# RWKV-7 time mixing: weight halves and modulation tiles issued in fixed slots behind each engine's last short operation

## The chip, the cores and the metric

The kernel runs on one NeuronCore of a Trainium2 chip. The metric is the device time of one execution in microseconds (us); the median of three runs before the change is 2659.18 us.

Engines as the profile names them: PE is the matrix engine (PEld its weight loads), DVE the vector engine, ACT the scalar engine, POOL is GpSimd, SP the queue that issues nearly all DMAs. PSUM is the memory PE writes to, SBUF the on-chip memory for everything else.

## The reference, cut to what matters

A trunk of two layers over 256 tokens of width 2048, all in float32. Layer 0 is RWKV-7 time mixing and a squared-ReLU MLP; layer 1 is attention and an MLP. Each sub-layer has a norm, a shift and scale from the conditioning vector `c`, and a gate. The change lies in layer 0's time mixing:

```python
mod = c @ w_ada[layer] + b_ada[layer]            # 12288 modulation values a layer, from a 2048 x 12288 matrix
sh1, sc1, gt1, sh2, sc2, gt2 = jnp.split(mod, 6, axis=-1)
...
xr, xw, xk, xv, xa, xg = [h + xx * mu[j] for j in range(6)]
r = xr @ w_r;  k = xk @ w_k;  v = xv @ w_v       # three 2048 x 2048 projections
...
def step(S, inp):                                # the recurrence of each of 32 heads, one token at a time
    r_t, w_t, k_t, v_t, kk_t, a_t = inp
    sa = jnp.einsum('bhvk,bhk->bhv', S, -kk_t)
    S = (S * w_t[:, :, None, :] + sa[..., None] * (kk_t * a_t)[:, :, None, :]
         + v_t[..., None] * k_t[:, :, None, :])
    return S, jnp.einsum('bhvk,bhk->bhv', S, r_t)
...
y = group_norm(y) + sum(r_h * k_h * r_k) * v_h
return (y * g) @ w_o
```

## The kernel before, in words

**Pairs and slots.** The 32 heads are worked as 16 pairs of two heads (128 channels). The recurrence is done in chunks of 64 tokens, so each pair needs a chain of small matrix products. Its work is a generator of 36 steps: `early` (8 steps: decay, key norm, scaled keys), `invert` (12 steps: the inverse of a triangular matrix, in levels l = 1 to 5, two steps a level) and `late` (16 steps: four chunks of three steps, then the group norm and gate). The loop at the end of `layer_a` runs over 164 slots, 8 a pair: in a slot each live pair takes one step, then PE gets a piece of dense work, two steps of the k and r projections of the next pair (12 matmuls of 128x256). In steady state four or five pairs are live, each at another place of its 36 steps. In this text phase 0 to 7 means the slot's number modulo 8, and a pair period is eight slots, from phase 0 to phase 0. One slot's results on ACT, DVE and POOL feed the next slot's matmuls.

**The short chains.** A step of `invert` transposes `u` on DVE (`tt`, line 243), PE multiplies it with a level mask of `als` (tile `al`), ACT copies the product (`xs`, line 247), PE multiplies that with `u`, and DVE adds the result to `u` (line 258). A chunk in `late` goes through PE, ACT (`g`, line 288; `sa`, line 292) and DVE (`zs`, lines 309 and 311).

**The long operations.** A float32 weight comes in halves of 512 KB (tile `raw`, a ring of 6 buffers), and is split in two parts: ACT casts it to `wH` (line 382), DVE subtracts for `wL` (line 385); `wH` and `wL` have 3 buffers each. The projections need four halves a pair (two of `w_k`, two of `w_r`); `self.weight` asks for both halves of a matrix at once, one matrix ahead. In the same slots the modulation vectors of later stages are computed: `self.ada()` takes one 512 KB tile of `w_ada` from the same ring of 6 and adds it, times a value of `c`, to an accumulator on DVE (`acc`, line 460; 458 for the first tile of 16), in phases 0, 1, 2, 4, 5, 6, from slot 16 on.

**What sets the order.** Each engine's instructions are ordered by a scheduler at build time, with priority for what was written first. `tc.issue_after(ins)` forces instructions of the same engine behind `ins`; before the change it is used for PE alone. Each engine works its own queue off in order. On PSUM the tile `ms` (two buffers) is shared by many short products: `z` (phase 0), the turned keys (1), the variance sums (1), the last inversion level (2 and 3), the key sums (2) and the gate (3).

Of the kernel before, what the change touches and what calls it, by code (L numbers as in the profile page):

```python
# [15 lines left out]
ALU = mybir.AluOpType  # L16
AX = mybir.AxisListType

P = 128
D = 2048  # L20
T = 256
KT = D // P
DFF = 8192
NQ = DFF // D
NPAIR = D // P
C = 64
H = C // 2
# [3 lines left out]
HK = 8  # L31
# [46 lines left out]
class Pair:  # L78
# [118 lines left out]
    def invert(self):  # L197
        b, nc, s, ch, kr, bh, kh = self.b, self.b.nc, self.s, self.ch, self.kr, self.bh, self.kh
        cst, pp = b.cst, b.pp

        def every(name):
            return cst(name).unsqueeze(1).to_broadcast([P, 4, H])

        def half(name, bufs):
            return b.pw.tile([P, 4, H], F32, tag=name, bufs=bufs, name=name)


        ui = cst("ui").unsqueeze(1).to_broadcast([P, 4, P])
        ts = []
        for src in (bh, kh):  # L210
            t = s()
            nc.gpsimd.tensor_tensor(out=ch(t), in0=ch(src), in1=self.pc.to_broadcast([P, 4, C]), op=ALU.mult)
            ts.append(t)
        pg = pp.tile([P, 4, P], F32, tag="gr", bufs=1, name="gr")
        self.each(lambda c: pg[:, c, :], lambda c: ch(bh)[:, c, :], lambda c: kr[:, c, :])
        ar = self.ar = s("ar", 3)
        nc.vector.tensor_tensor(out=ch(ar), in0=pg[:, :, C:P], in1=ui[:, :, C:P], op=ALU.mult)


        da, co, u = half("da", 1), half("co", 2), half("u", 2)  # L220
        for i, K in enumerate(QS):
            n = H * (i % 2)
            nc.scalar.copy(da[K], pg[K, :, n:n + H])
            if i % 2 == 0:
                nc.scalar.mul(co[K], pg[K, :, H:C], -1.0)
        nc.gpsimd.tensor_tensor(out=u, in0=da, in1=every("lev0"), op=ALU.mult)
        nc.gpsimd.tensor_tensor(out=u, in0=u, in1=every("eye_h"), op=ALU.add)
        als = b.pw.tile([P, 4, 4, H], F32, tag="al", bufs=2, name="al")
        nc.gpsimd.tensor_tensor(out=als, in0=da.unsqueeze(1).to_broadcast([P, 4, 4, H]),
                                in1=cst("levs").rearrange("p (l k) -> p l k", l=4).unsqueeze(2).to_broadcast([P, 4, 4, H]),  # L230
                                op=ALU.mult)
        yield
        pt = b.psm().rearrange("p (a c k) -> p a c k", a=2, c=4)
        for i, t in enumerate(ts):
            self.each(lambda c: pt[:, i, c, :], lambda c: ch(t)[:, c, :], lambda c: cst("eye"))
        bk = self.bk = b.pw.tile([P, 2, 4, C], F32, tag="bk", bufs=3, name="bk")
        nc.scalar.copy(bk, pt)
        yield
        uf = self.u = b.uf[self.j % 2]
        down, up = ((0, 1), (2, 3)), ((1, 0), (3, 2))  # L240
        for l in range(1, 6):
            tt_, xs = half("tt", 2), half("xs", 2)
            nc.vector.transpose(out=tt_.rearrange("p c t -> p (c t)"), in_=u.rearrange("p c t -> p (c t)"))
            pi = self.corner(l)
            if l < 5:
                self.tiles(pi, als[:, l - 1], tt_, [(i, i) for i in range(4)])
                nc.scalar.copy(xs, pi)
            else:
                self.tiles(pi, co, tt_, down)
                for i, K in enumerate(QS):  # L250
                    if i % 2:
                        nc.scalar.copy(xs[K], pi[K])
                    nc.gpsimd.tensor_copy(uf[K, :, H * (i % 2):H * (i % 2) + H], u[K])
            yield
            pi = self.corner(l)
            if l < 5:
                self.tiles(pi, xs, u, [(i, i) for i in range(4)])
                nc.vector.tensor_tensor(out=u, in0=u, in1=pi, op=ALU.add)
            else:
                self.tiles(pi, xs, u, up)  # L260
                for K in QS[::2]:
                    nc.scalar.copy(uf[K, :, H:C], pi[K])
            if l == 2:
                pg = pp.tile([P, 4, P], F32, tag="gr", bufs=1, name="gr")
                self.each(lambda c: pg[:, c, :], lambda c: ch(kh)[:, c, :], lambda c: kr[:, c, :])
                mk = self.mk = self.big("mk", 3)
                nc.vector.tensor_tensor(out=mk, in0=pg, in1=ui, op=ALU.mult)
            yield

    def late(self):  # L270
# [6 lines left out]
        zs = None  # L277
        for c in range(4):
            if c == 3:
                lg = pw.tile([P, 2, P], F32, tag="lg", bufs=1, name="lg")  # L280
                nc.sync.dma_start(out=lg, in_=b.d["lora2"][j, :, 2:4])
            g, sa = (pw.tile([P, C], F32, tag=n_, bufs=3, name=n_) for n_ in ("g", "sa"))
            for K in heads:
                mm(pch[K, 0, :], mk[K, c, 0:C], vp[K, c, :], start=True, stop=(c == 0))
            if c:
                for K in heads:
                    mm(pch[K, 0, :], kr[K, c, 0:C], zs[K, :], start=False, stop=True)
            nc.scalar.copy(g, pch[:, 0, :])
            yield
            for K in heads:  # L290
                mm(pch[K, 1, :], u[K, c, :], g[K, :], start=True, stop=True)
            nc.scalar.mul(sa, pch[:, 1, :], -1.0)
            yield
            for K in heads:
                mm(ch(py)[K, c, :], vp[K, c, :], mk[K, c, C:P], start=True, stop=False)
            if c:
                for K in heads:
                    mm(ch(py)[K, c, :], zs[K, :], kr[K, c, C:P], start=False, stop=False)
            for K in heads:
                ins = mm(ch(py)[K, c, :], sa[K, :], ch(ar)[K, c, :], start=False, stop=True)  # L300
            if c < 3:
                with b.tc.issue_after(ins.ins):
                    for K in heads:
                        mm(pch[K, 2, :], bk[K, 0, c, :], sa[K, :], start=True, stop=False)
                    for K in heads:
                        mm(pch[K, 2, :], bk[K, 1, c, :], vp[K, c, :], start=False, stop=True)
                zn = pw.tile([P, C], F32, tag="zs", bufs=4, name="zs")
                if c == 0:
                    nc.vector.tensor_copy(zn, pch[:, 2, :])
                else:  # L310
                    nc.vector.scalar_tensor_tensor(out=zn, in0=zs, scalar=pc[:, c, :], in1=pch[:, 2, :],
                                                   op0=ALU.mult, op1=ALU.add)
                zs = zn
            yield

# [18 lines left out]
class Body:  # L334
# [7 lines left out]
    def cst(self, name, rows=slice(None)):  # L342
        o, n = CST_AT[name]
        return self.csts[rows, o:o + n]
# [148 lines left out]
    def ada(self, n=1):  # L493
        for _ in range(n):
            self.ada_step()
        self.ada_fill()

    def last_pe(self):
        pe = self.nc.tensor.engine
# [140 lines left out]
    def layer_a(self, st, sp):  # L640
# [8 lines left out]
        with ExitStack() as s1:  # L649
# [137 lines left out]
            for n in range(KT):  # L787
# [19 lines left out]
                t = mixed(5, n, xx)  # L807
# [17 lines left out]
            for _ in range(2):  # L825
                v_part()
            s3.close()
            weights = iter([d[n][j] for j in range(NPAIR) for n in ("w_k", "w_r")])
            self.wnext = self.weight(next(weights))
            for i in range(4):  # L830
                nc.scalar.copy(v[:, 2 * i:2 * i + 2, :], pv[i])
            nc.scalar.activation(tw[:96, :], pl[0][:96, 0, :], AF.Tanh)
# [8 lines left out]
        with ExitStack() as s1:  # L841
# [13 lines left out]

            def proj_steps(pr):
                for dst, hl in (("k", xk), ("r", xr)):
                    w = self.wnext
                    src = next(weights, None)
                    self.wnext = None if src is None else self.weight(src)  # L860
                    ps = pp.tile([P, 2 * T], F32, tag="pj", bufs=2, name="pj")[:, :T]
                    for kt in range(KT):
                        self.proj(ps, w, lambda kt: hl[:, kt, :, 0:T], (kt, kt + 1))
                        if dst == "r" and kt == 1:
                            pr.lw = pw.tile([P, 2, P], F32, tag="lw", bufs=1, name="lw")
                            nc.sync.dma_start(out=pr.lw, in_=d["lora2"][pr.j, :, 0:2])
                        if kt % 2 == 1:
                            if kt == KT - 1:
                                t = pw.tile([P, T], F32, tag=dst, bufs=2, name=dst)
                                nc.scalar.copy(t, ps)  # L870
                                setattr(pr, dst, t)
                            yield
# [25 lines left out]
            for slot in range(S * NPAIR + Pair.STEPS):  # L898
# [24 lines left out]
                with tc.issue_after(last):  # L923
                    for _ in range(todo):
                        next(dense, None)
                if slot >= 2 * S and slot % 4 < 3:
                    self.ada()
            self.fin(HK)
        return v

# [311 lines left out]
```

## Time and profile before

| what | value |
|---|---|
| runs before | 2659.18, 2659.95, 2654.15 us (median 2659.18) |
| profiled execution | a span of 2653.8 us; no time of its own is given beside it |
| PE, DVE, ACT, POOL busy over the span | 97%, 79%, 52%, 8% |
| the loop over slots | from about 202 us to 733 us of the span; steady from 304 to 622 us |
| in the steady part (317.29 us) | PE busy 301.32, DVE 261.74, ACT 186.41, POOL 88.98 us |

How to read it: a row of the timeline has start, duration, engine, line, operation, output<-input, shape and count, and in brackets how long the engine sat idle before it and what ended that. A row of waits has who waited for whom, and then the us in total, how many times and the longest. A row of windows has the stretch, its length and each engine's busy time in it.

### The profile page before, as it was taken

The numbers are of one execution on the slowest core, as the hardware profiler recorded it, in microseconds if no ns is written. First come the engines' busy times: TensorE is split into PE (matmuls) and PEld (weight loads), VectorE is DVE, ScalarE is ACT, GpSimd is POOL, SyncE is SP. The second block draws the span as 40 slices with busy tenths as digits, with TensorE's granted clock in tenths as the row PEclk, the third lists the DMA queues.
The fourth block names the chain that finished last, engine by engine and source line by source line (L and its number), as shares of the span: only waits on it lengthen the run. The fifth ranks groups of instructions, "written<-read, shape, count | busy, mean of one in ns | idle before, by whom it ended". The sixth has DMA issues, their size and how long they took to land.

```text
span 2653.8 us, 59231 instructions
## 1 busy us (share of the span) xinstructions
PE 2574.9 (97%) x24108; PEld 2257.3 (85%) x24108; DVE 2089.4 (79%) x3054; ACT 1368.6 (52%) x2484; POOL 210.6 (8%) x338
## 2 busy tenths in 40 slices
PE   7999999999999999999999999999999999999997
PEld 4788888887899888888888998887898888888886
DVE  6888878878789888888888898899887556555555
ACT  3346555555456445355365554565564464453554
POOL 1002223223110000000001000000100000000002
PEclk9999999999999999999999999999999999999999
DMA  9976656565768888989888779887766555555553
GB/s 351 320 243 220 211 181 196 180 197 196 253 234 301 325 320 320 329 325 334 325 328 293 237 247 326 313 282 263 266 216 236 191 186 188 190 187 188 189 189 121
DMA packets 207664, 663.19 MB, mean 250 GB/s; under 512 B 21408, under 2 KB 55072, under 8 KB 207392
## 3 DMA queue, kind: packets, MB, share of 16 engines
q1 hardware_dynamic: 205328, 656.89, 71.7%
q8 instruction: 189, 3.10, 0.5%
q10 hardware_dynamic: 2064, 2.53, 0.3%
q14 instruction: 83, 0.68, 0.1%
HBM read 657.23 MB, written 2.10 MB: 248 GB/s over the span
## 4 chain that ended last, share of the span: by engine, by line
PE 84%; DVE 7%; issue 4%; DMA 3%; ACT 2%; POOL 1%; SPq 0%; DVEq 0%; ACTq 0%; POOLq 0%
PE pj L416 42%; PE pj L418 21%; PE pj L405 3%; PE pj L406 3%; PE pj L407 3%; DMA raw<-w_ada 2%; DVE wL L385 2%; DVE acc L460 1%; PE iv L111 1%; PE o L405 1%; PE ms L328 1%; PE o L407 0%; ACT wH L382 0%; PE o L406 0%; PE pT L1130 0%
## 5 line engine op out<-in xcount | busy, mean ns | idle before, releaser
L385 DVE TENSOR_TENSOR wL<-raw,wH 128x1024 fp32r<-128x1024 f32 x772 | 941.1, 1220 | 342.4 <-ACT wH L382 337.2
L382 ACT CAST wH<-raw 128x1024 fp32r<-128x1024 f32 x772 | 806.0, 1045 | 762.7 <-PE pj L416 590.2
L416 PE MATMUL pj<-aHL,wH 128*128 128x512 f32 x2816 | 893.3, 398 | 1.1 <-DVE x L955 1.1
L416 PE MATMUL pj<-hHL,wH 128*128 128x512 f32 x2048 | 644.7, 396 | 0.0
L418 PEld LDWEIGHTS pj<-aHL,wL 128*128 128x128 f32 x2816 | 531.7, 189 | 123.1 <-issue 0.3
L418 PE MATMUL pj<-aHL,wL 128*128 128x256 f32 x2816 | 564.1, 281 | 0.0
L418 PEld LDWEIGHTS pj<-hHL,wL 128*128 128x128 f32 x2048 | 384.5, 188 | 91.1 <-DVE wL L385 0.9
L416 PEld LDWEIGHTS pj<-aHL,wH 128*128 128x128 f32 x2816 | 432.1, 189 | 8.6 <-issue 8.3
L418 PE MATMUL pj<-hHL,wL 128*128 128x256 f32 x2048 | 402.6, 278 | 0.4 <-DVE wL L385 0.4
L460 DVE SCALAR_TENSOR_TENSOR acc<-rada,ct,acc 128x1024 f32<-128x1024 f32 x256 | 327.3, 1278 | 7.3 <-DMA rada<-w_ada 6.9
L416 PEld LDWEIGHTS pj<-hHL,wH 128*128 128x128 f32 x2048 | 312.2, 189 | 1.3 <-DVE hHL L1001 1.1
L405 PE MATMUL pj<-aHL,wH 128*128 128x256 f32 (+1 forms) x896 | 262.5, 293 | 0.0
L406 PE MATMUL pj<-aHL,wH 128*128 128x256 f32 (+1 forms) x896 | 254.2, 284 | 0.0
L407 PE MATMUL pj<-aHL,wL 128*128 128x256 f32 (+1 forms) x896 | 253.0, 282 | 0.0
L524 POOL TENSOR_TENSOR ss<-ss,sq 128x256 f32<-128x256 f32 x56 | 51.2, 915 | 1583.7 <-ACT sq L523 1583.4
L1026 DVE SCALAR_TENSOR_TENSOR x<-pj,mod,x 128x256 f32<-128x256 f32 x256 | 123.3, 482 | 64.2 <-PE pj L418 61.2
L405 PEld LDWEIGHTS pj<-aHL,wH 128*128 128x128 f32 x896 | 169.9, 190 | 4.5 <-issue 0.2
L407 PEld LDWEIGHTS pj<-aHL,wL 128*128 128x128 f32 x896 | 170.4, 190 | 0.4 <-DVE e L851 0.2
L406 PEld LDWEIGHTS pj<-aHL,wH 128*128 128x128 f32 x896 | 169.9, 190 | 0.5
L460 DVE SCALAR_TENSOR_TENSOR acc<-raw,ct,acc 128x1024 f32<-128x1024 f32 x104 | 138.0, 1327 | 17.4 <-DMA raw<-w_ada 17.2
L998 ACT ACTIVATE t<-t 128x256 f32<-128x256 f32 x112 | 46.9, 419 | 120.2 <-DVE t L970 120.2
L1001 DVE TENSOR_TENSOR hHL<-t,hHL 128x256 fp32r<-128x256 f32 x128 | 53.9, 421 | 1.7 <-ACT t L1000 1.0
(252 smaller groups left out, 2817.6 us busy)
## 6 DMA issues: line engine op xcount, KB each, us to landing
raw<-w_up SPq DMA_DIRECT2D x256, 512.0 KB, 4.0
raw<-w_down SPq DMA_DIRECT2D x256, 512.0 KB, 3.6
rada<-w_ada SPq DMA_DIRECT2D x209, 512.0 KB, 5.5
raw<-w_ada SPq DMA_DIRECT2D x111, 512.0 KB, 4.3
rada<-w_ada_kv SPq DMA_DIRECT2D x64, 512.0 KB, 6.6
rawa<-w_ada SPq DMA_DIRECT2D x32, 512.0 KB, 6.7
rawa<-w_ada_t SPq DMA_DIRECT2D x32, 512.0 KB, 7.1
raw<-w_k SPq DMA_DIRECT2D x32, 512.0 KB, 3.6
```

The lines of the kernel that those rows point to most:

```text
L382: nc.scalar.copy(Hf, raw)
L385: eng.tensor_tensor(out=Lf, in0=raw, in1=Hf, op=ALU.subtract)
L405: nc.tensor.matmul(ps, H[:, i, :], a(kt)[:, 0, :], start=(first and kt == 0), stop=False)
L406: nc.tensor.matmul(ps, H[:, i, :], a(kt)[:, 1, :], start=False, stop=False)
L407: ins = nc.tensor.matmul(ps, L[:, i, :], a(kt)[:, 0, :], start=False, stop=(last and kt == KT - 1))
L416: nc.tensor.matmul(ps, w[kt // HK][0][:, kt % HK, :], a(kt), start=(kt == 0), stop=False)
L418: ins = nc.tensor.matmul(ps[:, 0, :], w[kt // HK][1][:, kt % HK, :], a(kt)[:, 0, :], start=False, stop=(kt == KT - 1))
L460: nc.vector.scalar_tensor_tensor(out=self.acc, in0=raw, scalar=ck, in1=self.acc, op0=ALU.mult, op1=ALU.add)
L524: (eng or nc.gpsimd).tensor_tensor(out=self.ss, in0=self.ss, in1=sq, op=ALU.add)
L998: nc.scalar.activation(t, t, AF.Relu)
L1001: nc.vector.tensor_tensor(out=h[:, 1, :], in0=t, in1=h[:, 0, :], op=ALU.subtract)
L1026: nc.vector.scalar_tensor_tensor(out=x, in0=ps[:, i, :], scalar=self.mods[(layer, 5)][:, n:n + 1], in1=x, op0=ALU.mult, op1=ALU.add)
```

## The change

Seven edits, all in time mixing:

- In `invert` the transpose `tt` is issued at the end of the step that finishes `u`, not at the start of the step that uses it.
- On POOL the product `als` is forced behind the second operation on `u`.
- Short operations (`tt`, `xs`, `g`, `sa`, `zs`) are marked; `marks` holds the last one of each engine.
- `behind()` forces what is issued within it behind the marked operation of its engine. ACT and DVE have marks; SP and POOL have none.
- `w_load` keeps four raw halves loaded or on their way; `w_make` splits one and loads the next. `w_make` stands in phases 1, 3, 6 and 7, inside `behind()`.
- The projections take finished halves from a queue, two of which are made ahead of the loop.
- The modulation tiles move from phases 0, 1, 2, 4, 5, 6 to 0, 1, 2, 4, 6, 7, inside `behind()`. Their number stays 111.

```diff
-        nc.gpsimd.tensor_tensor(out=u, in0=u, in1=every("eye_h"), op=ALU.add)
+        ins = nc.gpsimd.tensor_tensor(out=u, in0=u, in1=every("eye_h"), op=ALU.add)
         als = b.pw.tile([P, 4, 4, H], F32, tag="al", bufs=2, name="al")
-        nc.gpsimd.tensor_tensor(out=als, in0=da.unsqueeze(1).to_broadcast([P, 4, 4, H]),
...
+        with b.tc.issue_after(ins.ins):
+            nc.gpsimd.tensor_tensor(out=als, in0=da.unsqueeze(1).to_broadcast([P, 4, 4, H]),
...
+        def turned():
+            t = half("tt", 2)
+            b.mark(nc.vector.transpose(out=t.rearrange("p c t -> p (c t)"), in_=u.rearrange("p c t -> p (c t)")))
+            return t
...
         nc.scalar.copy(bk, pt)
+        tt_ = turned()
         yield
...
-            tt_, xs = half("tt", 2), half("xs", 2)
-            nc.vector.transpose(out=tt_.rearrange("p c t -> p (c t)"), in_=u.rearrange("p c t -> p (c t)"))
+            xs = half("xs", 2)
...
-                nc.scalar.copy(xs, pi)
+                b.mark(nc.scalar.copy(xs, pi))
...
                 nc.vector.tensor_tensor(out=u, in0=u, in1=pi, op=ALU.add)
+                tt_ = turned()
...
-            nc.scalar.copy(g, pch[:, 0, :])
+            b.mark(nc.scalar.copy(g, pch[:, 0, :]))
...
-            nc.scalar.mul(sa, pch[:, 1, :], -1.0)
+            b.mark(nc.scalar.mul(sa, pch[:, 1, :], -1.0))
...
+                b.mark(ins)
                 zs = zn
...
+    def mark(self, ins):
+        self.marks[ins.ins.engine] = ins.ins
+
+    @contextmanager
+    def behind(self):
+        with ExitStack() as st:
+            for i in self.marks.values():
+                st.enter_context(self.tc.issue_after(i))
+            yield
+
+    def w_load(self):
+        src = next(self.w_src, None)
+        if src is not None:
+            self.w_raw.append(self.raw(src))
+
+    def w_make(self):
+        if self.w_raw:
+            self.w_made.append(self.halves(self.w_raw.popleft()))
+            self.w_load()
...
-            weights = iter([d[n][j] for j in range(NPAIR) for n in ("w_k", "w_r")])
-            self.wnext = self.weight(next(weights))
+            self.marks, self.w_raw, self.w_made = {}, deque(), deque()
+            self.w_src = iter([d[n][j][:, i * HK * P:(i + 1) * HK * P]
+                               for j in range(NPAIR) for n in ("w_k", "w_r") for i in range(KT // HK)])
+            for _ in range(4):
+                self.w_load()
+            for _ in range(2):
+                self.w_make()
...
-                    w = self.wnext
-                    src = next(weights, None)
-                    self.wnext = None if src is None else self.weight(src)
...
                     for kt in range(KT):
+                        if kt % HK == 0:
+                            w = [self.w_made.popleft()] * (KT // HK)
...
-                if slot >= 2 * S and slot % 4 < 3:
-                    self.ada()
+                with self.behind():
+                    if slot % S in (1, 3, 6, 7):
+                        self.w_make()
+                    if slot >= 2 * S and slot % S in (0, 1, 2, 4, 6, 7):
+                        self.ada()
```

What this moves is seen in the built order. On DVE, from the split keys of phase 0 (`ar`) of one pair period in the middle of the loop to the key squares (`sq`) that PE sums in phase 2; first before, then after (lines 460, 385, 258, 243 are 469, 394, 265, 236 after):

```order
L385 TENSOR_TENSOR wL<-raw,wH 128x1024
L217 TENSOR_TENSOR ar<-gr,csts 128x256
L138 TENSOR_SCALAR s_5673<-ms 128x512
L460 SCALAR_TENSOR_TENSOR acc<-raw,ct,acc 128x1024
L258 TENSOR_TENSOR u<-u,iv 128x128
L460 SCALAR_TENSOR_TENSOR acc<-raw,ct,acc 128x1024
L243 STREAM_TRANSPOSE tt<-u 128x128 x2
L311 SCALAR_TENSOR_TENSOR zs<-zs,pc,lt 128x64
L149 SCALAR_TENSOR_TENSOR s<-csts,s_5673 128x256
L460 SCALAR_TENSOR_TENSOR acc<-raw,ct,acc 128x1024
L125 TENSOR_TENSOR sq<-s,sq 128x256
```

The same stretch of DVE's queue in the changed kernel:

```order
L217 TENSOR_TENSOR ar<-gr,csts 128x256
L469 SCALAR_TENSOR_TENSOR acc<-raw,ct,acc 128x1024
L138 TENSOR_SCALAR s_5681<-ms 128x512
L469 SCALAR_TENSOR_TENSOR acc<-raw,ct,acc 128x1024
L265 TENSOR_TENSOR u<-u,iv 128x128
L236 STREAM_TRANSPOSE tt<-u 128x128 x2
L149 SCALAR_TENSOR_TENSOR s<-csts,s_5681 128x256
L319 SCALAR_TENSOR_TENSOR zs<-zs,pc,lt 128x64
L394 TENSOR_TENSOR wL<-raw,wH 128x1024
L125 TENSOR_TENSOR sq<-s,sq 128x256
```

The `acc` that stood between `u` and its transposes stands ahead of `u` now, with one more `acc` ahead of `s`; a `wL` stands ahead of `sq` where an `acc` stood. Other pair periods before have other orders; after, nearly all have this one.

On SP, which issues the loads, one pair period before:

```order
L372 DMA raw<-w_r 128x1024
L372 DMA raw<-w_ada 128x1024 x3
L372 DMA raw<-w_k 128x1024 x2
L372 DMA raw<-w_ada 128x1024 x2
L866 DMA lw<-lora 128x256
L372 DMA raw<-w_ada 128x1024
```

and after (line 372 is 381; the last row begins the next period):

```order
L381 DMA raw<-w_k 128x1024
L381 DMA raw<-w_ada 128x1024
L381 DMA raw<-w_k 128x1024
L381 DMA raw<-w_ada 128x1024 x2
L902 DMA lw<-lora 128x256
L381 DMA raw<-w_r 128x1024
L381 DMA raw<-w_ada 128x1024 x2
L381 DMA raw<-w_r 128x1024
L381 DMA raw<-w_ada 128x1024
L289 DMA lg<-lora 128x256
L381 DMA raw<-w_k 128x1024
```

Weight loads stood in twos and stand one by one now. A weight half's load stands a whole pair period ahead of its cast, so four of the six buffers of `raw` hold weights, and each `w_ada` load waits for the second-last long DVE operation, or the one before that, to free a buffer.

More of the change, by code (lines that the diff above doesn't have):

```diff
@@ L226, in invert @@
         nc.gpsimd.tensor_tensor(out=u, in0=da, in1=every("lev0"), op=ALU.mult)
-        nc.gpsimd.tensor_tensor(out=u, in0=u, in1=every("eye_h"), op=ALU.add)
+        ins = nc.gpsimd.tensor_tensor(out=u, in0=u, in1=every("eye_h"), op=ALU.add)
         als = b.pw.tile([P, 4, 4, H], F32, tag="al", bufs=2, name="al")
-        nc.gpsimd.tensor_tensor(out=als, in0=da.unsqueeze(1).to_broadcast([P, 4, 4, H]),
-                                in1=cst("levs").rearrange("p (l k) -> p l k", l=4).unsqueeze(2).to_broadcast([P, 4, 4, H]),
-                                op=ALU.mult)
+        with b.tc.issue_after(ins.ins):
+            nc.gpsimd.tensor_tensor(out=als, in0=da.unsqueeze(1).to_broadcast([P, 4, 4, H]),
+                                    in1=cst("levs").rearrange("p (l k) -> p l k", l=4).unsqueeze(2).to_broadcast([P, 4, 4, H]),
+                                    op=ALU.mult)
+        def turned():
+            t = half("tt", 2)
+            b.mark(nc.vector.transpose(out=t.rearrange("p c t -> p (c t)"), in_=u.rearrange("p c t -> p (c t)")))
+            return t
         yield
@@ L251, in invert @@
                     if i % 2:
-                        nc.scalar.copy(xs[K], pi[K])
+                        b.mark(nc.scalar.copy(xs[K], pi[K]))
                     nc.gpsimd.tensor_copy(uf[K, :, H * (i % 2):H * (i % 2) + H], u[K])
@@ L308, in late @@
                 if c == 0:
-                    nc.vector.tensor_copy(zn, pch[:, 2, :])
+                    ins = nc.vector.tensor_copy(zn, pch[:, 2, :])
                 else:
-                    nc.vector.scalar_tensor_tensor(out=zn, in0=zs, scalar=pc[:, c, :], in1=pch[:, 2, :],
-                                                   op0=ALU.mult, op1=ALU.add)
+                    ins = nc.vector.scalar_tensor_tensor(out=zn, in0=zs, scalar=pc[:, c, :], in1=pch[:, 2, :],
+                                                         op0=ALU.mult, op1=ALU.add)
+                b.mark(ins)
                 zs = zn
```

## The prediction

> **What bounds the kernel now.** I read the page's busy line first, then windows over the loop's pair periods, then the waits in its steady part, then the timeline around the longest waits.
>
> ```profile
> span 2653.8 us, 59231 instructions
> PE 2574.9 (97%) x24108; PEld 2257.3 (85%) x24108; DVE 2089.4 (79%) x3054; ACT 1368.6 (52%) x2484; POOL 210.6 (8%) x338
> ```
>
> PE is busy 97% of the span, so all that a change of order can win is the rest, or work that shows as busy only because a wait cut it. The change touches the loop alone. In the windows below each row is one pair period in the steady part (three of eleven, with their sum), then the ramp ahead of it and the tail behind it; the columns behind the length are busy times.
>
> ```profile
> core 0: us, PE busy (x) PEld busy (x) DVE busy (x) ACT busy (x) POOL busy (x), PEclk, DMA share, GB/s
> 332.47:363.11 30.64, 28.51 (x592) 25.62 (x591) 22.61 (x44) 16.68 (x47) 9.39 (x12) 0.94 0.52 167
> 507.32:535.14 27.82, 27.56 (x655) 24.99 (x654) 23.24 (x45) 16.67 (x47) 6.16 (x12) 1.00 0.51 161
> 563.81:593.86 30.05, 27.50 (x592) 24.52 (x591) 22.97 (x44) 16.46 (x47) 7.20 (x12) 1.00 0.56 170
> ...
> sum 317.29, PE 301.32 PEld 272.11 DVE 261.74 ACT 186.41 POOL 88.98; mean PE 27.39 PEld 24.74 DVE 23.79 ACT 16.95 POOL 8.09
> 229.42:304.48 75.06, 70.08 (x1529) 63.64 (x1528) 66.04 (x114) 42.98 (x110) 23.27 (x33) 1.00 0.69 218
> 621.77:733.00 111.23, 102.18 (x1750) 91.26 (x1750) 90.85 (x144) 54.70 (x139) 22.42 (x30) 0.95 0.72 239
> ```
>
> A pair period takes 317.29 / 11 = 28.84 us, the best 27.82, and the same program text gives both: the periods differ in how long operations happen to be ordered. PE sits idle 317.29 - 301.32 = 16.0 us in the eleven, 75.06 - 70.08 = 5.0 in the ramp, 111.23 - 102.18 = 9.1 in the tail: 30 us, 1.1% of the span, bounds any gain. (The first row's granted clock of 0.94 makes it longer by some 1.8 us of its own; the change has no part in that.) DVE is busy 23.79 of 28.84, so it is the next bound, 5 us behind.
>
> Who keeps PE waiting, and who keeps its feeders waiting, over those eleven periods:
>
> ```profile
> PE ms L328 <- DVE s L158: 3.1, 4, 1.1
> PE ms L111 <- ACT sl L323: 3.1, 2, 1.9
> PE iv L111 <- DVE tt L243: 2.1, 4, 0.7
> PE ms L116 <- ACT sl L322: 1.5, 3, 0.6
> PE ms L111 <- DVE tt L243: 1.2, 1, 1.2
> PE ms L116 <- DVE sq L125: 1.0, 1, 1.0
> ACT wH L382 <- PE pj L406: 24.6, 31, 1.3
> DVE acc L460 <- DMA raw<-w_ada: 13.9, 15, 2.1
> DVE tt L243 <- POOL u L227: 5.3, 6, 0.9
> ```
>
> PE's waits all come from DVE, or from ACT operations that are fed by DVE, in phases 1 to 4. The lower three rows are the long operations: ACT stands 24.6 us in front of casts whose `wH` buffer PE still reads, and DVE 13.9 us in front of `acc` whose tile has not landed. While an engine stands there, the short operations queued behind stand too. One place shows it, on DVE and then on PE:
>
> ```profile
> 396.63 1.28 DVE L460 SCALAR_TENSOR_TENSOR acc<-raw,ct,acc 128x1024 f32<-128x1024 f32 x1 [2.12 <-DMA raw<-w_ada]
> 397.84 0.28 DVE L258 TENSOR_TENSOR u<-u,iv 128x128 f32<-128x128 f32 x1
> 398.61 1.28 DVE L460 SCALAR_TENSOR_TENSOR acc<-raw,ct,acc 128x1024 f32<-128x1024 f32 x1 [0.49 <-DMA raw<-w_ada]
> 399.81 0.50 DVE L243 STREAM_TRANSPOSE tt<-u 128x128 f32<-128x128 f32 x2
> ...
> 402.16 0.42 DVE L125 TENSOR_TENSOR sq<-s,sq 128x256 fp32r<-128x256 f32 x1
> ...
> 405.23 0.41 DVE L158 TENSOR_SCALAR s<-ms 128x256 f32<-128x256 f32 x1
> ...
> 400.26 0.35 PE L111 MATMUL ms<-tt,co 32*32 32x32 f32 x11 [1.16 <-DVE tt L243]
> 402.63 0.38 PE L116 MATMUL ms<-sq,bones 128*128 128x256 f32 x1 [1.00 <-DVE sq L125]
> 405.70 1.13 PE L328 MATMUL ms<-tg,lg 128*128 128x256 f32 x4 [0.61 <-DVE s L158]
> ```
>
> `u` is done at 398.12, yet `tt` starts at 399.81: 1.69 us for an `acc` between them and its DMA. PE then waits 1.16, 1.00 and 0.61 us in a row as DVE is late from there on.
>
> **The change part by part.** It adds and removes no arithmetic: 64 halves and 111 modulation tiles as before, and a mark is no instruction.
>
> *Transposes behind `u`.* At the quoted place `tt` comes 1.69 us earlier. The PE rows that wait for `tt` hold 2.1 + 1.2 = 3.3 us over the eleven periods; I take all of it, ends 0 and 3.3.
>
> *`als` behind `u` on POOL.* These are four POOL rows, of two periods:
>
> ```profile
> 395.70 1.10 POOL L229 TENSOR_TENSOR al<-da,csts 128x512 f32<-128x512 f32 x1
> 396.75 1.45 POOL L227 TENSOR_TENSOR u<-u,csts 128x128 f32<-128x128 f32 x1
> ...
> 425.75 2.09 POOL L229 TENSOR_TENSOR al<-da,csts 128x512 f32<-128x512 f32 x1
> 427.79 0.43 POOL L227 TENSOR_TENSOR u<-u,csts 128x128 f32<-128x128 f32 x1
> ```
>
> `u` comes 1.10 to 2.09 us earlier, so the 5.3 us that DVE stood for it go. On PE this counts only through `tt`, above. `als` itself ends 0.43 us later at least and is first read in phase 2; it is hidden as long as it ends there, 2 us or so after the `u` of today.
>
> *Casts at fixed places.* A `wH` buffer is free when its cast is reached: at phase 1 the third buffer holds r's second half of the last pair, which PE left at phase 7. The 24.6 us of ACT go, and `xs`, `g`, `sa` no longer queue behind a cast. PE hardly waits for ACT directly, so I take nothing for this beyond DVE's row below. If the cover goes, PE lacks a half: each is made two or three slots of 3.6 us (28.84 / 8) ahead of its use, against 1.2 us for either operation on it, so nothing is late. What is queued behind: in the built order the cast of phase 1 stands right behind `sa` and ahead of the copies `da` that POOL turns into `u`, so these come up to 1.2 us later; the 1.10 us or more that POOL gains cover that, and without them `tt` would lose it.
>
> *DMAs.* SP has no mark; its loads wait for buffers only. Four of the six `raw` buffers hold weights now, so a modulation load starts when the long DVE operation one or two places earlier is done. That makes a chain through DVE and DMA: load, `acc`, load, `acc`. In the built order each pair period has four such loads in series (those of phases 4, 6, 7, 1), with the other operations between them on DVE. Durations, and DMA issue to landing, in the same part of the trace:
>
> ```profile
> L385 DVE TENSOR_TENSOR wL<-raw,wH 128x1024 fp32r<-128x1024 f32 x43 | 52.6, 1222 | 10.8 <-ACT wH L382 9.5 <-DMA raw<-w_k 1.2
> 424.86 0.68 DVE L138 TENSOR_SCALAR s<-ms 128x512 f32<-128x512 f32 x1
> 433.65 0.47 DVE L329 SCALAR_TENSOR_TENSOR sl<-v,vecs,sl 128x256 f32<-128x256 f32 x1
> raw<-w_ada SPq DMA_DIRECT2D x67, 512.0 KB, 4.1
> raw<-w_r SPq DMA_DIRECT2D x20, 512.0 KB, 4.8
> ...
> 446.16 0.71 PE L482 MATMUL ms<-csts,acc 128*32 128x1 f32 x64
> ```
>
> Six `acc` of 1.28, one `wL` 1.22, `s` 0.68, `sl` 0.47, `s` (line 158) 0.41: 10.5 us, and 0.1 for each load's two hand-overs (a guess; ends 0 and 0.3): 10.9. Three loads at 4.1 and the one that is issued right behind a `w_r` load at 4.8: 17.1. The chain takes 28.0 us a period, 0.84 less than now. With all four at 4.8 it takes 30.1, with all at 3.5 it takes 24.9 and PE is the bound again: the best period (27.82, with 0.26 idle) says 27.56 for PE. Of that 0.7 is the last row, 64 small matmuls at the end of a modulation vector's half, which one period in 16 / 6 = 2.7 has (the count in its row is 64 above the next row's); so PE takes 26.85 + 0.27 = 27.1 on average.
>
> The Trainium skill's page "DMA: Bandwidth & Descriptors", sections "Bandwidth" and "Latency and other measured facts", gives about 2 us of fixed cost a DMA and a fabric ceiling of 435 GB/s. That is an estimate of 3.2 us for a 512 KB tile and a chain of 23.7 us, under PE's own time. The trace's 4.1 us is longer, with loads that overlap, and the measurement decides.
>
> *Sum.* Steady part 11 x 0.84 = 9.2 us. Of the ramp's 5.0 I take 1, a fifth, as its last period is like the steady ones; of the tail's 9.1 none, since no weight is made there by the new rule. Together 10.2 us, so the profiled execution's span of 2653.8 would be 2643.6. The runs' median stands 5.4 above that span, which the change leaves alone: 2659.2 - 10.2 = 2649.
>
> **The rivals.**
>
> *The loads land sooner and every wait goes.* With loads spread one by one, 3.5 us each would free DVE, and the periods fall to PE's 27.1: 11 x 1.74 = 19 us, with 3 from ramp and tail 2637. For it: the loads of today come in bursts. Against: even the best period has 27.82.
>
> *The loads get later: slower.* Two buffers for the modulation tiles instead of what was free of six. The chain passes today's 28.84 when the four loads average (28.84 - 10.9) / 4 = 4.5 us. With all four at the 4.8 of the `w_r` row it takes 30.1, and the eleven periods are 11 x 1.26 = 14 us slower: 2673. For it: DVE waits for these tiles 13.9 us even now, and order alone decides. Against: bursts of loads become rarer.
>
> *POOL's `als` holds up DVE.* It moves to where `tt`, `zs` and `wL` stand on DVE. The POOL rows above show that POOL stretches beside an `acc`: 1.10 to 2.09, 0.43 to 1.45. If DVE is what waits instead, it loses up to 1.10 us a period ahead of `sq`, 12 us in all, which takes the whole gain: 2661, no change. The Trainium skill's page "SBUF — State Buffer", section "SBUF: two separate sides", says so: the two share a port pair as an exclusive lock, whoever starts first holds it for the whole instruction, against a DVE operation with two SBUF inputs. The stretched POOL rows agree; no row here shows DVE losing a whole `als`.
>
> *The waits only move.* PE's largest row, for `s` (line 158), has an `acc` ahead of it in the new order too, and phases 0 to 3 hold four `acc` after. If what `tt` gains is lost there, 3 us or less remain: 2656.
>
> **How the numbers follow.** Forecast 0.42; sooner 0.13; later 0.17; `als` 0.10; moved 0.18. A measurement of this kernel can tell 0.2%, 5.3 us. Faster is the forecast and the first rival, 0.55; same is `als` and moved, 0.28; slower 0.17. The range goes from 2636, just under the first rival, to 2672, just short of later's price, so that half of each of these two is left out (0.15) and the rest is in; the forecast's own range is 2643 to 2654.
>
> **What would show it.** Right: the rows of PE waiting for `tt` gone, `tt` within 0.1 us of `u`'s end, the cast's wait for PE gone, pair periods alike at 27.5 to 28.4 us, and DVE's waits for `raw<-w_ada` still 10 us or more, in phases 6, 7 and 0. Wrong: `raw<-w_ada` landing in 5 us or more with PE waiting for `tt` at phase 4, behind the `acc` of phase 2; or the steady periods at 28.8 with PE's waits on lines 328 and 116 larger than before.

## The result, and the profile after

The changed kernel takes 2680.94 us (median of 4 runs, 2675.53 to 2686.74) against 2658.22 for the kernel before in the same session: a ratio of 1.0085, 95% interval 1.0065 to 1.0105. It is slower, and outside the range of 2636 to 2672. The profiled execution (2676.78 us) opens with these two lines of its page:

```profile
span 2675.0 us, 59142 instructions
PE 2584.9 (97%) x24108; PEld 2264.3 (85%) x24108; DVE 2094.6 (78%) x3054; ACT 1367.6 (51%) x2484; POOL 219.3 (8%) x338
```

The span grew by 21.2 us. Windows of the changed kernel, cut as before: four of the eleven pair periods with the sum over all eleven, then the ramp and the tail (length, busy time of PE, PEld, DVE, ACT and POOL, then granted clock, DMA share and GB/s):

```profile
338.19:367.07 28.88, 27.24 (x591) 24.39 (x590) 24.14 (x44) 16.42 (x47) 10.41 (x12) 1.00 0.66 205
367.07:401.16 34.09, 29.52 (x656) 26.94 (x655) 24.73 (x45) 16.75 (x47) 8.27 (x12) 0.90 0.51 162
429.74:463.30 33.56, 27.31 (x591) 24.40 (x591) 26.38 (x46) 17.16 (x48) 8.33 (x12) 1.00 0.63 197
582.39:610.76 28.37, 27.11 (x591) 24.36 (x590) 25.54 (x45) 16.54 (x47) 9.30 (x12) 1.00 0.65 199
...
sum 331.87, PE 307.56 PEld 276.60 DVE 271.49 ACT 185.26 POOL 98.75; mean PE 27.96 PEld 25.15 DVE 24.68 ACT 16.84 POOL 8.98
229.42:309.57 80.15, 70.77 (x1522) 64.24 (x1518) 63.18 (x109) 41.64 (x109) 23.38 (x33) 0.98 0.63 195
641.44:754.20 112.76, 104.22 (x1749) 92.83 (x1749) 91.78 (x145) 55.23 (x140) 21.19 (x30) 0.94 0.74 244
```

The ramp is 5.1 us longer than before (80.15 - 75.06), the eleven periods 14.6 (331.87 - 317.29), the tail 1.5 (112.76 - 111.23): the whole 21.2. Of the 14.6 us in the steady part PE's idle time is 8.3 (24.3 against 16.0). The other 6.2 are PE busy time (307.56 against 301.32), for the same matmuls: a lower clock. It was 0.90 in the second row, 0.89 and 0.94 in two periods that are not shown, and 1.00 in the others; before, one period had 0.94 and the others 1.00. By these shares the low clock takes some 6.7 us more than before, an estimate that fits the 6.2. The periods are not alike either. The quiet ones run from 28.37 to 28.88 us, and two take 34. Nor is their order: in the trace, seven of the eleven have the order on DVE that is shown for the changed kernel, from `ar` to `sq`. The waits of those eleven periods:

```profile
PE ms L491 <- DVE acc L469: 12.5, 4, 4.8
PE ms L337 <- DVE s L158: 5.8, 7, 1.1
PE ms L111 <- DVE tt L236: 0.6, 2, 0.4
ACT wH L391 <- PE pj L415: 0.3, 1, 0.3
DVE acc L469 <- DMA raw<-w_ada: 21.6, 27, 2.4
```

and the loads of the modulation tiles between 300 and 645 us (KB each, median us from issue to landing; before 4.1):

```profile
raw<-w_ada SPq DMA_DIRECT2D x73, 512.0 KB, 3.9
```

The two waits that the change was about are gone from the steady part: PE for `tt` (3.3 us, now 0.6) and ACT's cast for PE (24.6, now 0.3). In the ramp PE's wait for `tt` grew, from 4.2 us for this pair of tiles to

```profile
PE iv L111 <- DVE tt L236: 6.5, 4, 2.7
```

At the longest place there `u` is done at 263.97 and `tt` starts at 266.11: an `s` and an `acc` still stand between them.

The first row of the steady part's waits is new. Line 491 is the 64 small matmuls that sum a finished modulation vector's half (line 482 before, where no such row stood): PE now stands there up to 4.8 us at a time. One of these places, in DVE's, POOL's, SP's and PE's timelines:

```profile
372.14 2.15 DVE L469 SCALAR_TENSOR_TENSOR acc<-raw,ct,acc 128x1024 f32<-128x1024 f32 x1 [0.97 <-DMA raw<-w_ada]
374.22 0.28 DVE L265 TENSOR_TENSOR u<-u,iv 128x128 f32<-128x128 f32 x1
374.53 0.50 DVE L236 STREAM_TRANSPOSE tt<-u 128x128 f32<-128x128 f32 x2
...
375.82 1.21 DVE L394 TENSOR_TENSOR wL<-raw,wH 128x1024 fp32r<-128x1024 f32 x1
...
377.72 0.47 DVE L333 SCALAR_TENSOR_TENSOR sl<-lt,vecs,sl 128x256 f32<-128x256 f32 x1
378.11 1.35 DVE L469 SCALAR_TENSOR_TENSOR acc<-raw,ct,acc 128x1024 f32<-128x1024 f32 x1
...
372.10 1.11 POOL L230 TENSOR_TENSOR al<-da,csts 128x512 f32<-128x512 f32 x1
...
374.32 3.10 SPq L381 DMA_DIRECT2D raw<-w_ada  x2
...
374.76 0.28 PE L416 MATMUL pj<-aHL,wL 128*128 128x256 f32 x1
379.61 1.04 PE L491 MATMUL ms<-csts,acc 128*32 128x1 f32 x64 [4.57 <-DVE acc L469]
...
382.69 0.41 PE L414 MATMUL pj<-aHL,wH 128*128 128x256 f32 x1
```

`tt` starts 0.03 us after `u` ends, as forecast. But the last `acc` of the vector comes only at 378.11, and two things hold it there at once. In DVE's order it stands behind `tt`, `s`, `zs`, `wL`, `sq`, `kr` and `sl`, and DVE works without a pause from 374.22 on. And SP issues the load of its tile at 374.32, just as the `acc` before it ends (374.29), so that with the median of 3.9 us the tile would land at about 378.2 (an estimate). The `acc` has no wait for a DMA in its row, so this place does not tell the two apart. DVE was late ahead of it too: the `acc` at 372.14 waited 0.97 us for its load and took 2.15 us instead of some 1.28, with `al` running on POOL beside it. At the other long stand the load came last:

```profile
461.87 1.28 DVE L469 SCALAR_TENSOR_TENSOR acc<-raw,ct,acc 128x1024 f32<-128x1024 f32 x1 [2.37 <-DMA raw<-w_ada]
463.31 0.87 PE L491 MATMUL ms<-csts,acc 128*32 128x1 f32 x53 [4.76 <-DVE acc L469]
```

In PE's queue the sums come ahead of the next slot. So PE has nothing to do from 375.04 to 379.61 although `tt`, which the next short products read, is done at 375.03. After that the 128x256 matmul takes 0.41 us where it took 0.28.

### The profile page after: what moved, and what is told of

Same layout as the page of the kernel before. It is cut to its first block, busy times and chain, and to the rows that moved or that the text cites. A ratio compares the mean times of both kernels' runs of the same rounds, so it can differ in the third digit from the quotient of the medians.

```text
span 2675.0 us, 59142 instructions
## 1 busy us (share of the span) xinstructions
PE 2584.9 (97%) x24108; PEld 2264.3 (85%) x24108; DVE 2094.6 (78%) x3054; ACT 1367.6 (51%) x2484; POOL 219.3 (8%) x338
## 4 chain that ended last, share of the span: by engine, by line
PE 83%; DVE 7%; DMA 5%; issue 3%; ACT 2%; POOL 0%; DVEq 0%; ACTq 0%; SPq 0%; POOLq 0%
PE pj L425 42%; PE pj L427 21%; DMA raw<-w_ada 4%; PE pj L414 3%; PE pj L415 3%; PE pj L416 3%; DVE acc L469 2%; DVE wL L394 2%; PE iv L111 1%; ACT wH L391 1%; PE gr L105 1%; PE o L414 1%; PE ms L337 1%; PE m L730 0%; PE pT L1169 0%
```

## The experiments

All on the kernel before or after, each timed against the kernel before on the same chip. Two theories were set against each other first. A: PE's stand at the sums is the loss. B: the loss is a chain of loads through the two `raw` buffers that four waiting weight halves leave free. Rows of waits and groups below are those between 300 and 645 us of each span, nearly the eleven periods.

**The sums read a constant tile.** Left out: the values of the modulation vectors finished in the loop come out of constants.

```diff
+        acc = self.csts if self.sum_const else acc      # first line of ada_sum; set within the loop only
```

> The changed kernel, but inside the slot loop the 64 small matmuls that sum a finished modulation vector read the constants instead of the accumulator (the modulation values of layer 0's gate and MLP then come out of constants): same instructions, but PE no longer waits there for the vector's last acc. Theory A (PE's queue stands at these sums for an acc that is now held behind the short operations, and the clock drops after the long stands): the 15.7 us of PE idle on that line go and most of the extra low-clock stretches with them, 2652 to 2660 us. Theory B (two buffers for the modulation tiles make a chain of loads that paces DVE): the sums are only where the lateness shows; 2670 us or more.

2662.26 us, ratio 1.0017 (1.0003 to 1.0030). PE's row at line 491 is gone, DVE's wait stays:

```profile
DVE acc L469 <- DMA raw<-w_ada: 23.5, 28, 2.7
```

The time lies between the two expectations, close to A's. The stand is worth 0.7% (1.0085 to 1.0017), but without it the kernel is still no faster than before.

**Two halves ahead instead of four.**

```diff
-            for _ in range(4):
+            for _ in range(2):
                 self.w_load()
```

> The changed kernel, but two raw weight halves are kept loaded ahead instead of four, so four of the six raw buffers serve the modulation tiles. Theory A: the acc stays behind the short operations, only its DMA wait shrinks; PE still stands at most sums; 2665 to 2678 us. Theory B: DVE's waits for raw<-w_ada (21.6 us between 300 and 645 us) fall under 5 us and the loop gets its forecast pace of 28 us a pair; 2648 to 2656 us.

2652.71 us, ratio 0.9982 (0.9968 to 0.9996), as B has it. DVE no longer waits for any modulation load, as the group of the 71 `acc` shows (busy and mean, then idle ahead of them); the stand at the sums, in the waits below it, shrinks but stays:

```profile
L469 DVE SCALAR_TENSOR_TENSOR acc<-raw,ct,acc 128x1024 f32<-128x1024 f32 x71 | 93.2, 1312 | 0.0
```

```profile
PE ms L491 <- DVE acc L469: 5.0, 3, 2.1
```

**The sums one modulation slot later.**

```diff
+            self.lazy = True                            # ahead of the loop; False again behind it
```

> The changed kernel, but a vector's sums are issued one modulation slot later, at the first tile of the next vector, so PE reaches them after the last acc has long run. The next vector's first acc must then wait for the sums on DVE, some 2 us in seven places. Theory A: PE's waits on the sums' line fall under 3 us; 2655 to 2663 us. Theory B: no better than 2670 us.

2665.02 us, ratio 1.0028 (1.0015 to 1.0040), between the two expectations. PE's wait at the sums falls from 12.5 to

```profile
PE ms L491 <- DVE acc L469: 1.6, 2, 0.9
```

**Both: two halves ahead and late sums.**

> Both of the last two: two raw halves ahead and the sums one modulation slot later. Theory A: like the late sums alone, 2652 to 2662 us. Theory B: like two halves ahead alone, 2648 to 2656 us. If both count, it is the fastest of the four and below the kernel before, 2645 to 2652 us.

2641.12 us, ratio 0.9940 (0.9921 to 0.9958): faster than either kernel and than every expectation, with a span of 2636.8. Neither wait has a row any more. So A and B both hold: each repair alone brings the kernel back to about the old time, both together pass it. Late sums alone take 0.6% off the changed kernel's time, two halves alone 1.0%, both 1.45%, nearly the sum.

**What makes the stand: tiles not held.** The modulation tiles taken out of `behind()`, the halves left in.

```diff
                 with self.behind():
                     if slot % S in (1, 3, 6, 7):
                         self.w_make()
-                    if slot >= 2 * S and slot % S in (0, 1, 2, 4, 6, 7):
-                        self.ada()
+                if slot >= 2 * S and slot % S in (0, 1, 2, 4, 6, 7):
+                    self.ada()
```

> The changed kernel with the modulation tiles in the new phases but no longer held behind the marks (the weight halves stay held). Theory A, that PE stands at a vector's sums because its last acc is held behind the slot's marked short operations: the stands of 4.6 to 4.8 us at line 491 shrink to 2 us or less and about 16 us come back, 2664. Theory B, that an acc comes late because its load starts late (four of the six raw buffers hold weights), and the marks do not matter: DVE still waits some 20 us for raw<-w_ada, the stands stay at 10 us or more together, and the time stays within 5 us of 2680.

2682.97 us, ratio 1.0084 (1.0062 to 1.0105): nothing came back, as theory B has it.

```profile
DVE acc L469 <- DMA raw<-w_ada: 28.7, 25, 2.3
PE ms L491 <- DVE acc L469: 10.9, 3, 5.5
```

The first theory's cause falls: it is not the marks alone. Not held, the vector's last `acc` still stands behind `wL`, `sq`, `kr` and `sl` in DVE's order (at 380.98, ahead of the longest stand), and the loads are late as before.

**Tiles in the old slots**, held: `slot % 4 < 3` in place of the list.

> The changed kernel with the modulation tiles held behind the marks, but in the slots of before (0, 1, 2 of each four instead of 0, 1, 2, 4, 6, 7 of eight). Theory B with the chain of loads: the gaps between the tiles are as many, DVE's wait for raw<-w_ada stays at 15 to 25 us in the loop and the time within 6 us of 2680. Rival C, that it is the new phases 6, 7, 0, 1, 2 in a row that outrun two buffers: with pauses at 3 and 7 the wait falls under 10 us and the time to 2665 or less.

2668.67 us, ratio 1.0042 (1.0027 to 1.0057). Half of the loss is back, but neither expectation fits: DVE waits more than with the new slots, not less, and PE's stand is nearly as long.

```profile
DVE acc L469 <- DMA raw<-w_ada: 29.2, 32, 2.1
PE ms L491 <- DVE acc L469: 10.8, 4, 3.4
```

Why this order loses less is not settled: PE's row for `s`, 5.8 us in the changed kernel, is gone here, which is not tested by itself. Each edit also lets the scheduler order the whole loop anew, so some tenths of a per cent can come of an order that the edit did not aim at; no run here measures how much. With four free buffers the slots make no difference that shows (below).

**The transposes and `als` alone**, on the kernel before: `tt` right behind `u`, `als` behind `u`; weights and tiles as before.

> The kernel before with the first part of the change alone: tt issued right behind u, and als behind u on POOL; weights and modulation tiles as before. By the prediction's term the 3.3 us of PE's waits for tt in the steady part go, and up to 4 more in the ramp (7.9 over the loop): 2651 to 2655. Rival, als beside DVE's operations costs up to 1.1 us a pair: 2658 to 2669.

2658.11 us, ratio 1.0007 (0.9997 to 1.0017): no gain. But most of the wait stays as well, 2.6 us in its two rows against 3.3 before:

```profile
PE iv L111 <- DVE tt L236: 1.6, 3, 1.0
PE ms L111 <- DVE tt L236: 1.0, 1, 1.0
```

`tt` is written right behind `u`, but it is not issued there. With nothing held, the scheduler still puts long operations between them:

```profile
403.92 0.27 DVE L265 TENSOR_TENSOR u<-u,iv 128x128 f32<-128x128 f32 x1
404.12 1.27 DVE L469 SCALAR_TENSOR_TENSOR acc<-raw,ct,acc 128x1024 f32<-128x1024 f32 x1
405.31 0.49 DVE L236 STREAM_TRANSPOSE tt<-u 128x128 f32<-128x128 f32 x2
```

An `acc` or a `wL` stands between a `u` and the next `tt` at 12 places from 305 to 645 us; it is 13 in the kernel before and none in the changed one. So this run does not show what early transposes are worth by themselves. A loss by `als` does not show either, 0.17% at most.

**Late sums on the kernel before**, as a control (the edit of the third experiment):

> The kernel before with each vector's sums one modulation slot later. It is the control for the late sums: if they help only where an acc is held back, nothing moves here (2655 to 2660), since no wait of PE for acc at the sums' line shows in the trace of before; if spreading the sums is worth something by itself, it gains the same 0.5% as in the changed kernel, 2644.

2659.39 us, ratio 1.0006 (0.9996 to 1.0015): late sums are worth something only where the change made an `acc` late.

**Three halves ahead** (`range(3)`), otherwise as changed:

> The changed kernel with three weight halves held ahead in raw buffers instead of four, so that three buffers are left for the modulation tiles. With four it took 1.0085 of the kernel before, with two 0.998. If the loss is a chain through two buffers (a load starts when the load before it has landed and the acc two places earlier is done), the third buffer breaks it, most of the loss goes and SP's wait for raw<-w_ada to land with it: 0.998 to 1.001, 2653 to 2660. If it is a matter of how many bytes are under way, it lies in the middle: 1.002 to 1.005, 2663 to 2671.

2649.91 us, ratio 0.9970 (0.9960 to 0.9979). One buffer more does all that two did, and more than the expectation said: it is the chain, not the number of loads under way. SP's waits for a modulation load to land, before, after, and here, then DVE's and PE's here:

```profile
SPq L372 <- DMA raw<-w_ada: 31.4, 15, 6.1
```

```profile
SPq L381 <- DMA raw<-w_ada: 60.0, 39, 4.4
```

```profile
SPq L381 <- DMA raw<-w_ada: 17.9, 15, 2.1
DVE acc L469 <- DMA raw<-w_ada: 1.4, 3, 0.7
PE ms L491 <- DVE acc L469: 7.0, 4, 2.3
```

**The fastest version with nothing held** (two ahead, late sums, same slots, but no `behind()`):

> The fastest version so far (two halves ahead, sums one modulation slot later; 2641, 0.994) with the same slots for halves and tiles, but no longer held behind the marks. If the holding itself is worth something, the short operations wait for casts and acc again and 3 to 10 us are lost: 2644 to 2651. If only the slots count, as in the comparison with freed tiles in the changed kernel, nothing moves: 2638 to 2644.

2658.04 us, ratio 1.0003 (0.9994 to 1.0012): all of its gain is lost, more than either side expected. The waits of before are back, and that for `tt` is longer than it was:

```profile
ACT wH L391 <- PE pj L415: 23.3, 28, 1.3
DVE acc L469 <- DMA raw<-w_ada: 20.2, 16, 2.8
PE iv L111 <- DVE tt L236: 7.7, 9, 2.2
```

**The fastest version with the first part undone** (`tt` in the slot that reads it, `als` ahead of `u`):

```diff
-            xs = half("xs", 2)
+            tt_, xs = half("tt", 2), half("xs", 2)
+            b.mark(nc.vector.transpose(out=tt_.rearrange("p c t -> p (c t)"), in_=u.rearrange("p c t -> p (c t)")))
...
-                nc.vector.tensor_tensor(out=u, in0=u, in1=pi, op=ALU.add)
-                tt_ = turned()
+                b.mark(nc.vector.tensor_tensor(out=u, in0=u, in1=pi, op=ALU.add))
```

> The fastest version so far with the first part of the change undone: tt is written again in the slot that reads it, and als ahead of u on POOL (the marks stand on u's addition and on tt). Alone on the kernel before, that part moved nothing (1.0007). If it is worth nothing here too, 2638 to 2644. Rival: it matters once halves and tiles are held, since tt then stands behind a whole acc and wL of the slot before: 2646 to 2656, with PE waiting for tt 5 us or more over the loop.

2662.52 us, ratio 1.0018 (1.0008 to 1.0028). The rival is right, and its price was too low:

```profile
PE iv L111 <- DVE tt L243: 12.0, 13, 1.2
```

The cause is the one that the rival names: before PE's matmul at 364.74, which waited 0.97 us, DVE ran an `acc` (361.49), `v`, a `wL` (363.15) and only then `tt` (364.29), and ten other places are alike. The part that gained nothing alone is worth 0.8% once long operations are held in place (0.9940 to 1.0018). The run undoes `als` too, and DVE's `tt` stands 10.1 us for POOL's `u` in it; what each of the two is worth was not tested apart.

**The fastest version with the tiles in the old slots:**

> The fastest version so far with the modulation tiles in the slots of before (0, 1, 2 of each four). In the changed kernel that gave back half of the loss (1.0085 to 1.0042). If the new slots are bad only by the chain through two buffers, nothing moves here, where four buffers are free: 2638 to 2645. If the new slots cost something by themselves, this is faster by 3 to 10 us: 2631 to 2638.

2638.87 us, ratio 0.9930 (0.9914 to 0.9945); its interval overlaps that with the new slots. With four free buffers the slots make no difference that shows.

**Three ahead, tiles not held, halves held, sums at their old place:**

> Three halves ahead, and the modulation tiles no longer held behind the marks (the halves stay held). With three ahead and held tiles it took 0.997, with 9.6 us of PE's waits for acc at the sums left in the loop. If the holding makes that stand, as the prediction's reader would think from the order, the 9.6 us go and it takes 0.993 to 0.995 (2639 to 2644). If the holding is worth more than the stand costs (in the fastest version halves and tiles freed together lost 0.6%), the short operations wait again and it takes 0.998 to 1.002 (2652 to 2663).

2660.99 us, ratio 1.0013 (1.0001 to 1.0025). PE's row at the sums, 7.0 us with three ahead and the tiles held, is gone: that rest of the stand comes from the holding. (With three ahead and the tiles held, `wL` and `sq` stand ahead of the last `acc` at the stand of 2.26 us that ends at 365.94, and that `acc` waits for no DMA.) But more is lost elsewhere: with nothing holding them, DVE reaches its `acc` ahead of their loads again, though three buffers are free:

```profile
SPq L381 <- DMA raw<-w_ada: 72.1, 40, 3.3
DVE acc L469 <- DMA raw<-w_ada: 33.9, 30, 2.5
```

These waits make no stand at the sums here, while the 28.7 us of the kernel with freed tiles and two buffers do. The traces show a difference of order: at the first of these sums the vector's last `acc` stands ahead of `u` here (364.36, with the sums at 367.10), and behind `wL`, `sq`, `kr` and `sl` there (380.98). Why the scheduler chose two places for it is open.

**Three ahead, late sums, old slots:**

> Three halves ahead, sums one modulation slot later, tiles in the slots of before: the three repairs that each took time away from the changed kernel, together. With two halves ahead they gave 0.993. If three buffers suffice for the tiles, 0.992 to 0.994 (2636 to 2642); if the chain of loads still binds a little (DVE waited 2.7 us for raw<-w_ada with three ahead), 0.995 to 0.997 (2644 to 2650).

2642.64 us, ratio 0.9951 (0.9939 to 0.9964), between the two expectations: DVE still waits a little for `raw<-w_ada` (4.8 us), and its interval touches that of the same version with two halves (0.9914 to 0.9945). Three halves ahead are no better than two.

## Why the prediction was wrong

*What bounds the kernel* was right as far as it went: order alone, and DVE as the one PE waits for.

*The step that failed first: the vector sums.* The prediction counted the 64 small matmuls as 0.7 us of PE time, spread over 2.7 periods. It never asked what they wait for and what is queued behind them on PE, though it did ask this of casts and of `als`. In the order before, `acc` was early enough that no row showed; the change put the vector's last `acc` behind a later load and behind a `wL` and short operations on DVE: at 461.87 the load came last, at 378.11 the two fell together. 12.5 us of PE standing in the steady part were the price, and 0.7% of the time by the experiment with constant sums. No rival named this place.

*The chain of loads* was the right mechanism with a wrong size. It was seen ("that makes a chain through DVE and DMA"), with 28.0 us a period, below the old 28.84. The quiet periods take 28.37 to 28.88, so as a period without a sum it was 0.4 to 0.9 short, though the loads landed sooner than the 4.1 us it was worked out with: 3.9. The larger error was to price the chain as a mean. Its end is a late `acc`, and where that `acc` is a vector's last one PE stands, up to 4.8 us at a time. The term gave a gain of 9.2 us; broken by one more buffer, it gives back 1.15% (1.0085 to 0.9970), about 31 us, the smaller stand included.

*The clock.* The prediction put a period's lower clock aside: "the change has no part in that". It had: PE's busy time in the steady part grew by 6.2 us, and around the ends of both long stands the clock was at half.

*The transposes* (3.3 us, all taken): in the steady part the wait went, in the ramp it grew, and the time got longer. Alone, this part reads 1.0007, but there most of the wait stayed, since writing `tt` early did not make the scheduler issue it early. In the fastest version undoing it, `als` with it, costs 0.8%. So its worth depended on what else was held, and the 3.3 us of waits in the kernel before could not show it.

*Casts at fixed places* (nothing taken): the 24.6 us of ACT did go. What holding is worth cannot be read in the changed kernel, where it is drowned; in the fastest version it is 0.6%, with the tiles held too.

*The tail* (0) lost 1.5 us and *the ramp* (a gain of 1) lost 5.1. The ramp was taken as like the steady part, but PE's waits for `tt` grew there by 2.9 us (4.2 + 0.7 before, 6.5 + 1.3 after).

*The rivals.* "The loads get later: slower" had the right side, a price of 2673 and, in the two buffers that it names, the right place, as the third buffer shows; but it priced loads that land in 4.8 us, and they landed in 3.9. "`als` holds up DVE": an `acc` beside it is stretched, to 2.15 us at the quoted stand, but in the kernel before too (1.91 at 484.30), and the mean of all `acc` hardly moved (1335 to 1346 ns). "The waits only move" is true of the row for `s` (3.1 to 5.8), a small part. The signs named beforehand came out mixed: `tt`, cast and DVE's wait for `raw<-w_ada` (21.6) as said; periods alike at 27.5 to 28.4 not. Of the signs of being wrong, the longer wait on line 328 came (337 now, 3.1 to 5.8 us), with a mean period of 30.2 us (331.87 / 11).

## What to carry to other kernels

When long operations get fixed places, list every matmul that reads one of their results, and what stands behind that matmul in PE's queue: a small sum at the end of an accumulation can stop the engine that bounds the kernel. Prefetch depth is taken from somebody: four halves ahead in a ring of six cost 1.15% against three, for no lead that was needed. And do not judge the parts of such a change one by one, nor by the program's text: late sums moved nothing on the kernel before, and transposes written early were not issued early there, while with halves and tiles held and buffers free late sums are worth 0.4%, early transposes with `als` 0.8%, and the whole beats the old kernel by 0.6 to 0.7%.

## What the runs showed of the hardware

PE's granted clock fell to half after several of its stands of 2 us and more, for longer than the stand had lasted. Around the end of the stand of 4.57 us (379.61) the changed kernel's clock was 0.50 in this window:

```profile
378.00:384.80 6.80, 5.19 (x132) 5.03 (x133) 3.67 (x7) 2.23 (x7) 1.81 (x2) 0.50 0.74 231
```

With three halves ahead, a stand of 2.26 us was enough:

```profile
365.94 0.70 PE L491 MATMUL ms<-csts,acc 128*32 128x1 f32 x64 [2.26 <-DVE acc L469]
```

Windows of the same kernel around it:

```profile
363.68:366.97 3.29, 1.03 (x105) 1.04 (x106) 3.29 (x6) 1.09 (x3) 3.13 (x5) 1.00 0.52 179
366.97:370.38 3.41, 3.41 (x51) 3.23 (x34) 2.07 (x5) 2.00 (x7) 0.77 (x2) 0.50 0.81 250
370.38:373.79 3.41, 3.41 (x69) 2.79 (x68) 2.58 (x8) 1.61 (x5) 0.00 (x0) 1.00 0.20 64
```

PE was busy 1.03 of 3.29 us, and the next 3.41 us ran at half the clock; with a full queue that is 1.7 us of work less, an estimate. So this stand cost nearly twice its length, which a count of idle time does not see. Not every stand is followed by it: in the changed kernel PE stood 2.72 us up to 266.56 and 2.18 us up to 620.90, and the clock stayed at 1.00 (in the windows 263.50:274.00 and 618.00:630.00). The Trainium skill's page "TensorE: Matmul & The Clock Gate", section "Part 1: The HAM clock gate", says that a free-running window of about 3.4 us sets the clock, and that it falls after at least one idle window. The length of 3.41 us agrees; that a whole idle window is needed does not, since this one held 1.03 us of work.
